# A one-layer decoder trunk on one core: activations' buffers moved by 32 bytes, two weight loads placed behind VectorE's splits, and a last addition cut in two ahead of the final vector's products

## The chip, the cores and the metric

The kernel runs on one core of one Trainium2 chip. The metric is the device time of one execution in microseconds (us). Before the change the median of three runs is 1251.67 us (1251.46 to 1252.79). Differences of about 0.2%, some 2.5 us, are what a measurement of this kernel can tell from no change.

## The reference, cut to what matters

One layer over 256 tokens of width 2048, all in float32:

```
h = rms_norm(x, g_mix);  q,k,v of three head groups = split(h @ w_in)
x += concat(diff_attn(6 heads), block_attn(4), dilated(6)) @ w_out
x += cross_attention(rms_norm(x, g_cross), rms_norm(mem, g_mem)) @ w_co
g, u = split(rms_norm(x, g_ffn) @ w_up)          # 2 x 5632 columns
x += (silu(causal_conv3(g) + b) * u) @ w_down    # 5632 rows
out = rms_norm(x, g_final)
```

Nearly all of the work is the weight matrices: each is read once from HBM and multiplied with 256 tokens.

## The kernel before, in words

**Precision.** Every factor of a product is held as a pair, `hi` and `lo`, in a rounded float32 format (fp32r in the profile): `hi` is the rounded value and `lo` the remainder. A product is then three matmuls: hi by hi, hi by lo, lo by hi. ScalarE makes `hi` of the weights (a copy, L142) and VectorE makes `lo` (a subtraction, L149). The text calls the two together a split.

**Pieces and steps.** The weights come in pieces of 1 MB, each loaded by one DMA of the queue of SP into one of four buffers `raw` (L127). A piece has two halves; half number i is used in step i of the main loop, so that piece k serves the steps 2k and 2k+1. In step i the loop first issues the splits of half i+4 (ScalarE's copy, then work queued for "before step i", then VectorE's subtraction), then TensorE's matmuls of half i, and then work queued for "after step i". Each engine carries out its instructions in just the order in which they are issued, so a split that waits for its load holds up all that is behind it on ScalarE and on VectorE.

**Who stands still in a matmul.** A TensorE matmul loads one factor (the stationary one, 128x128) and streams the other (the moving one). In the products with `w_in`'s q and k columns, `w_out`, `w_cq`, half of `w_ckv` and `w_up`, the weights are stationary and the activations `hT` move: per 128x128 weight block one matmul of 512 columns (L295: `hi` against hi and lo of the activation, side by side) and one of 256 (L302: `lo` against the activation's hi). With `w_co` it is three of 256 columns (L297, L298, L302). For the v columns the activations are stationary and the weights move (L341 to L343, 512 or 256 columns), and in the last product, with `w_down`, the activations `ah` and `al` are stationary and the weights move (L851 to L853, 512 columns). In the cross attention both factors are activations (L401).

**Where the buffers lie.** Each buffer starts at a multiple of 32 bytes in its partition. The weights' buffers `hi`, `lo` and `raw` start at multiples of 64 (`hi` at 67520, 71616 and so on, `lo` at 88000 and so on). Between them and the activations lie many small buffers. `hT` starts at 117856 and 150624, `ah` at 210016, `al` at 214112, all 32 bytes past a multiple of 64, and so do the cross attention's `qk`.

**The start.** By hand, ahead of the loop: x is loaded in pieces between the halves of weight pieces 0, 1 and 2, the splits of halves 0 and 1 are issued, and after steps 0 to 5 come the activations of two more row blocks (`put_x`: L194 on ScalarE, L197 on VectorE) and the splits of halves 2 to 7. The loop itself issues the splits from half 8 on: half 8 in step 4, ahead of `put_x` of the blocks 12 and 13 and of the split of half 6, which come after step 4. A fourth `raw` buffer, `hold`, is set on GpSimd and read by VectorE before step 8, so that no load takes it until then. Piece 3 goes to piece 0's buffer and piece 4 to piece 1's, each when VectorE has split the piece that lay there.

**Evacuation.** A group of four products (4 banks of PSUM) ends every eighth step; its sums leave by a ScalarE copy (L354) and a VectorE addition (L355). Five banks serve the products with `w_in`, so that from its second column group on, the next step's matmuls wait for these.

**The end.** The last two row blocks of `w_down` are kept back, so that the eight column blocks of the output (2 token tiles t, 4 blocks n) end one after another. For each, VectorE adds the residual (L890), ScalarE squares and sums (`square_sum`), and VectorE multiplies with g_final (L898). When all four are in, L899 to L901 add the sums, GpSimd raises to the power -0.5 (L903), and `finish` scales and stores each block.

Of the kernel before, what the change touches and what calls it, by code (L numbers as in the profile page):

```python
# [25 lines left out]
KF = DFF // P  # L26
# [8 lines left out]
HALF = 1024  # L35
NRAW = 4
# [26 lines left out]
def trunk(ctx, tc, x, mem, w_in, w_out, diff_lambda, rel_bias_table, w_cq, w_ckv, w_co, w_up, conv, w_down,  # L63
          g_final, onehot, biasadd, out):
    nc = tc.nc
    PE, DVE, ACT, POOL, SP = nc.tensor, nc.vector, nc.scalar, nc.gpsimd, nc.sync
# [3 lines left out]
    wpool = ctx.enter_context(tc.tile_pool(name="wpool", bufs=1))  # L70
# [35 lines left out]
    pieces = []  # L106
# [6 lines left out]
    def new_raw(p):  # L113
        if p.raw is None:
            p.raw = wpool.tile([P, 2 * HALF], F32, tag="raw", name="raw", bufs=NRAW)

    def load(p):
        new_raw(p)
        at = 0
        for src in p.srcs:  # L120
            n = 1
            for _, c in src.ap[1:]:
                n *= c
            dst = p.raw[:, at:at + n]
            if len(src.ap) == 3:
                dst = dst.rearrange("p (k n) -> p k n", k=src.ap[1][1])
            SP.dma_start(dst, src)  # L127
            at += n
        assert at == 2 * HALF
# [9 lines left out]
    def split_hi(p, h):  # L139
        hi = wpool.tile([P, HALF], F32R, tag="hi", name="hi", bufs=NSPLIT)  # L140
        lo = wpool.tile([P, HALF], F32R, tag="lo", name="lo", bufs=NSPLIT)
        ACT.copy(hi, p.raw[:, h * HALF:(h + 1) * HALF])  # L142
        p.parts[h] = (hi, lo)
        if p.extra is not None and h == 0:
            p.extra[0]()

    def split_lo(p, h):
        hi, lo = p.parts[h]
        DVE.tensor_tensor(lo, p.raw[:, h * HALF:(h + 1) * HALF], hi.bitcast(F32), op=ALU.subtract)  # L149
        if p.extra is not None and h == 0:  # L150
            p.extra[1]()
# [6 lines left out]
    def before(i, f):  # L158
        pre.setdefault(i, []).append(f)

    def after(i, f):
        post.setdefault(i, []).append(f)
# [13 lines left out]
    mhalf = cst.tile([P, 1], F32, name="mhalf")  # L176
# [30 lines left out]
    def xblock(k):  # L207
        return xT[:, k, :]
# [444 lines left out]
    for h in range(HA):  # L653
        i = startA + (0, 6, 11, 17, 22, 28)[h]
# [5 lines left out]
    for j in range(HB):  # L660
        i = startB + (1, 3, 4, 6)[j]
# [161 lines left out]
    def xtok(t, c):  # L823

        return xT[:, 4 * c + 2 * t:4 * c + 2 * t + 2, :].rearrange("p k n -> p (k n)")
# [5 lines left out]
    outs = {}  # L831
    parts = {}
    TAIL = 2
# [9 lines left out]
        hi, lo = parts[k]  # L843
        DVE.tensor_tensor(lo, ffn["a"][:, k, :], hi.bitcast(F32), op=ALU.subtract)

    def down_mm(p, k, h, t, n):
        hi, lo = p.parts[h]
        ah, al = (a[:, t * P:(t + 1) * P] for a in parts[k])
        o = outs[t, 2 * h + n]
        wh, wl = hi[:, n * 512:(n + 1) * 512], lo[:, n * 512:(n + 1) * 512]  # L850
        PE.matmul(o, ah, wh, start=(k == 0), stop=False)  # L851
        PE.matmul(o, ah, wl, start=False, stop=False)  # L852
        PE.matmul(o, al, wh, start=False, stop=(k == KF - 1))  # L853

    ss3 = small(8, "ss3", 1)
    fin = {}

    def finish(n, t, og, r):
        col = slice(n * 512, (n + 1) * 512)
        if t and n % 2:  # L860
            DVE.scalar_tensor_tensor(og[:, col], xtok(t, n), r, gfin["t"][:, col], op0=ALU.mult, op1=ALU.mult)
        elif t or n < 2:
            ACT.activation(og[:, col], og[:, col], AF.Copy, scale=r)
        else:
            (DVE, POOL)[n - 2].tensor_scalar_mul(og[:, col], og[:, col], r)
        SP.dma_start(out[t * P:(t + 1) * P, col], og[:, col])

    def down(k):
        def f(p, h):
            if k == 0 and h == 0:  # L870
                for t in range(NT):
                    for n in range(4):
                        outs[t, n] = any_tile()
            fin[k] = p
            if k < KF - TAIL:
                for t in range(NT):
                    for n in range(2):
                        down_mm(p, k, h, t, n)
            elif k == KF - 1 and h == 1:
                done = None  # L880
                for t in range(NT):
                    og = wpool.tile([P, 2 * HALF], F32, tag="raw", name="raw", bufs=NRAW)
                    ms = small(2, "msf")
                    ss = ss3[:, 4 * t:4 * t + 4]
                    for n in range(4):
                        for kk in range(KF - TAIL, KF):
                            down_mm(fin[kk], kk, n // 2, t, n % 2)
                        col = slice(n * 512, (n + 1) * 512)
                        xc = xtok(t, n)
                        DVE.tensor_tensor(xc, outs[t, n], xc, op=ALU.add)  # L890
                        square_sum(xc, ss[:, n:n + 1])
                        if done:
                            for m in ((3, 0, 1), (2,), (), ())[n]:
                                finish(m, *done)
                        gains = ((), (0,), (), (2,)) if t else ((0,), (1,), (2,), (3,))
                        for m in gains[n]:
                            col = slice(m * 512, (m + 1) * 512)
                            DVE.tensor_tensor(og[:, col], xtok(t, m), gfin["t"][:, col], op=ALU.mult)  # L898
                    DVE.reduce_sum(ms[:, 0:1], ss[:, :3], axis=AX.X)  # L899
                    DVE.tensor_scalar(ms[:, 0:1], ms[:, 0:1], 1.0 / D, EPS, op0=ALU.mult, op1=ALU.add)  # L900
                    DVE.scalar_tensor_tensor(ms[:, 1:2], ss[:, 3:4], 1.0 / D, ms[:, 0:1], op0=ALU.mult, op1=ALU.add)  # L901
                    r = small(1, "rfin")
                    POOL.tensor_tensor(r, ms[:, 1:2], mhalf, op=ALU.pow)  # L903
                    done = t, og, r
                for n in range(4):
                    finish(n, *done)
        return f
# [5 lines left out]
    gfin = {}  # L913
# [8 lines left out]
    def load_x(a, n):  # L922
        c = slice(GCOLS + a * S if a else 0, GCOLS + (a + n) * S)
        SP.dma_start(xin[:, c], x[:, c])

    def load_block(eng, p, k):
        new_raw(p)
        src = p.srcs[0]
        eng.dma_start(p.raw[:, k * 512:(k + 1) * 512],
                      bass.AP(tensor=src.tensor, offset=src.offset + k * src.ap[1][0],  # L930
                              ap=[list(src.ap[0]), list(src.ap[2])]))
# [1 line left out]
    load_x(0, 2)  # L933
    load_block(ACT, pieces[0], 0)
    load_block(SP, pieces[0], 1)
    ACT.copy(small(1, "first", 1), mhalf)
    load_x(2, 2)
    load_half(pieces[0], 1)
    load_x(4, 2)
# [4 lines left out]
    load_half(pieces[2], 0)  # L944
    load_half(pieces[2], 1)
    load_x(12, 4)

    hold = wpool.tile([P, 2 * HALF], F32, tag="raw", name="raw", bufs=NRAW)  # L950
    POOL.memset(hold[:, :1], 0.0)
    before(8, lambda: DVE.tensor_copy(small(1, "held", 1), hold[:, :1]))


    warm = acc_tile()
# [5 lines left out]
    def put_x(k):  # L961
        for f in (high, low):
            for j in range(2):
                f(xblock(k + j), MIX, lambda: hT["h"], k + j)

    def split(i):
        split_hi(pieces[i // 2], i % 2)
        split_lo(pieces[i // 2], i % 2)

    put_x(0)  # L970
    p = pieces[0]
# [5 lines left out]
    put_x(2)  # L977
    split(1)
    load(pieces[3])
    nload = 4  # L980
    for i in range(6):
        after(i, lambda i=i: (put_x(2 * i + 4), split(i + 2)))
    for c in range(4):
        square_part(c + 5, "x", c, lambda c=c: xpart(c))
    norm_factors(10, "x")
# [36 lines left out]
    nsplit = 8  # L1022
    for i in range(2 * len(pieces)):
        cur[0] = i
        new = []
        while nsplit < min(2 * len(pieces), i + 1 + LEAD if i > 2 else 0):
            while nload < len(pieces) and nload <= nsplit // 2 + NRAW - 2:
                load(pieces[nload])
                nload += 1
            new.append((pieces[nsplit // 2], nsplit % 2))  # L1030
            nsplit += 1
        for p, h in new:
            split_hi(p, h)
# [39 lines left out]
```

## Time and profile before

The profile is of one execution of 1252.27 us. Its span, from the first to the last instruction, is 1250.5 us, so 1.77 us lie around it; it is 0.60 us above the median of the runs.

| | |
|---|---|
| median of three runs | 1251.67 us |
| profiled execution | 1252.27 us, span 1250.5 us, mean granted TensorE clock 0.995 |
| matmuls | 6928, busy 1235.8 us |
| VectorE, ScalarE busy | 830.8 us, 630.0 us |
| HBM read | 230 MB, 186 GB/s over the span |

A row of the view of groups gives the source line, engine, operation, `out<-in` by the program's names, sizes, count, then busy time, the mean of one in ns and the idle time ahead. A row of the timeline gives start and duration in us, the instruction, and in brackets how long the engine was idle before it and what ended that. [...]

### The profile page before, as it was taken

The numbers are of one execution on the slowest core, as the hardware profiler recorded it, in microseconds if no ns is written. First come the engines' busy times: TensorE is split into PE (matmuls) and PEld (weight loads), VectorE is DVE, ScalarE is ACT, GpSimd is POOL, SyncE is SP. The second block draws the span as 40 slices with busy tenths as digits, with TensorE's granted clock in tenths as the row PEclk, the third lists the DMA queues.
The fourth block names the chain that finished last, engine by engine and source line by source line (L and its number), as shares of the span: only waits on it lengthen the run. The fifth ranks groups of instructions, "written<-read, shape, count | busy, mean of one in ns | idle before, by whom it ended". The sixth has DMA issues, their size and how long they took to land.

```text
span 1250.5 us, 17611 instructions
## 1 busy us (share of the span) xinstructions
PE 1235.8 (99%) x6928; PEld 1072.4 (86%) x6928; DVE 830.8 (66%) x1351; ACT 630.0 (50%) x979; POOL 12.3 (1%) x23
## 2 busy tenths in 40 slices
PE   8999999999999999999999999999999999999997
PEld 7888888988888899888888888888888888888885
DVE  5755676576568877876767768667776854445445
ACT  6544555556455656545445444444444544444444
POOL 0000000000000000000000000000000000000000
PEclk9999999999999999999999999999999999999998
DMA  7855554555566555565556565565556555555541
GB/s 275 273 172 191 189 170 159 182 184 156 177 227 217 170 169 164 204 206 169 170 201 196 175 202 190 183 201 184 187 180 202 192 193 180 200 176 194 187 150 68
DMA packets 104835, 233.26 MB, mean 187 GB/s; under 512 B 4208, under 2 KB 14768, under 8 KB 98992
## 3 DMA queue, kind: packets, MB, share of 16 engines
q1 hardware_dynamic: 104576, 231.85, 55.3%
q8 instruction: 54, 0.88, 0.3%
q10 hardware_dynamic: 144, 0.26, 0.1%
q14 instruction: 29, 0.24, 0.1%
q0 software_dynamic: 32, 0.02, 0.0%
HBM read 230.00 MB, written 2.12 MB: 186 GB/s over the span
## 4 chain that ended last, share of the span: by engine, by line
issue 58%; PE 37%; DMA 2%; DVE 2%; ACT 0%; POOL 0%; DVEq 0%; POOLq 0%; SPq 0%; ACTq 0%
PE acc L295 16%; PE acc L302 8%; PE acc L341 3%; PE acc L343 3%; PE acc L342 3%; DMA raw<-in_w_in 1%; PE at L401 1%; DMA xin<-in_x 1%; DVE lo L149 1%; PE at L420 0%; PE at L444 0%; DVE hT L197 0%; PE acc L298 0%; PE acc L297 0%; PE at L472 0%
## 5 line engine op out<-in xcount | busy, mean ns | idle before, releaser
L149 DVE TENSOR_TENSOR lo<-raw,hi 128x1024 fp32r<-128x1024 f32 x423 | 517.1, 1223 | 360.0 <-ACT hi L142 359.5
L142 ACT CAST hi<-raw 128x1024 fp32r<-128x1024 f32 x423 | 442.8, 1048 | 473.1 <-PE acc L295 272.4
L295 PE MATMUL acc<-hT,hi 128*128 128x512 f32 x1776 | 625.4, 395 | 3.5 <-ACT hi L142 3.3
L302 PE MATMUL acc<-hT,lo 128*128 128x256 f32 x1840 | 512.0, 280 | 0.6 <-DVE lo L149 0.6
L295 PEld LDWEIGHTS acc<-hT,hi 128*128 128x128 f32 x1776 | 334.4, 188 | 78.1 <-ACT hi L142 3.7
L302 PEld LDWEIGHTS acc<-hT,lo 128*128 128x128 f32 x1840 | 345.3, 188 | 1.4 <-DVE lo L149 1.2
L295 PE MATMUL at<-hT,hi 128*128 128x512 f32 x528 | 187.5, 392 | 0.0
L302 PE MATMUL at<-hT,lo 128*128 128x256 f32 x528 | 147.6, 280 | 0.0
L295 PEld LDWEIGHTS at<-hT,hi 128*128 128x128 f32 x528 | 99.1, 188 | 21.8
L302 PEld LDWEIGHTS at<-hT,lo 128*128 128x128 f32 x528 | 99.2, 188 | 0.0
L851 PE MATMUL acc<-hi,ah 128*128 128x512 f32 x220 | 87.8, 399 | 0.0
L853 PE MATMUL acc<-hi,al 128*128 128x512 f32 x220 | 86.7, 394 | 0.0
L852 PE MATMUL acc<-lo,ah 128*128 128x512 f32 x220 | 86.2, 392 | 0.0
L341 PE MATMUL acc<-hi,hT 128*128 128x256 f32 (+1 forms) x224 | 75.0, 335 | 0.0
L343 PE MATMUL acc<-hi,hT 128*128 128x256 f32 (+1 forms) x224 | 73.9, 330 | 0.0
L342 PE MATMUL acc<-lo,hT 128*128 128x256 f32 (+1 forms) x224 | 73.8, 330 | 0.0
L851 PE MATMUL at<-hi,ah 128*128 128x512 f32 x132 | 52.7, 399 | 0.0
L853 PE MATMUL at<-hi,al 128*128 128x512 f32 x132 | 52.0, 394 | 0.0
L788 ACT ACTIVATE y<-y 128x256 f32<-128x256 f32 x44 | 18.4, 419 | 66.3 <-DVE y L784 66.3
L852 PE MATMUL at<-lo,ah 128*128 128x512 f32 x132 | 51.7, 392 | 0.0
L853 PEld LDWEIGHTS acc<-hi,al 128*128 128x128 f32 x220 | 41.3, 188 | 10.8
L852 PEld LDWEIGHTS acc<-lo,ah 128*128 128x128 f32 x220 | 41.3, 188 | 9.8
(159 smaller groups left out, 1003.2 us busy)
## 6 DMA issues: line engine op xcount, KB each, us to landing
raw<-in_w_up SPq DMA_DIRECT2D x88, 1024.0 KB, 5.0
raw<-in_w_in SPq DMA_DIRECT2D x45, 1024.0 KB, 5.2
raw<-in_w_down SPq DMA_DIRECT2D x44, 1024.0 KB, 4.9
raw<-in_w_out SPq DMA_DIRECT2D x12, 1024.0 KB, 5.3
raw<-in_w_ckv SPq DMA_DIRECT2D x8, 1024.0 KB, 5.6
raw<-in_w_out SPq DMA_DIRECT2D x8, 512.0 KB, 4.9
raw<-in_w_cq SPq DMA_DIRECT2D x4, 1024.0 KB, 5.3
raw<-in_w_co SPq DMA_DIRECT2D x4, 1024.0 KB, 5.2
```

The lines of the kernel that those rows point to most:

```text
L142: ACT.copy(hi, p.raw[:, h * HALF:(h + 1) * HALF])
L149: DVE.tensor_tensor(lo, p.raw[:, h * HALF:(h + 1) * HALF], hi.bitcast(F32), op=ALU.subtract)
L295: PE.matmul(accs[n], w, x, start=(i == 0), stop=False)
L302: PE.matmul(accs[n][:, :S], lo[:, j, n * P:(n + 1) * P], src()[:, korder[i], :S], start=False, stop=(i == len(korder) - 1))
L341: PE.matmul(o, xh, hi[:, j, :], start=(i == 0), stop=False)
L342: PE.matmul(o, xh, lo[:, j, :], start=False, stop=False)
L343: PE.matmul(o, xl, hi[:, j, :], start=False, stop=(i == len(korder) - 1))
L401: PE.matmul(out, a[u], b[w], start=first and i == 0, stop=last and i == 2)
L788: after(cur[0] + 1 + n, lambda: ACT.activation(gate[k], gate[k], AF.Silu))
L851: PE.matmul(o, ah, wh, start=(k == 0), stop=False)
L852: PE.matmul(o, ah, wl, start=False, stop=False)
L853: PE.matmul(o, al, wh, start=False, stop=(k == KF - 1))
```

## The change

Three parts.

1. `ss3` grows from 8 to 10 floats and `first` from 1 to 16, and `held` is gone. With that `hT` starts at 117888 and 150656, `ah` at 210048, `al` at 214144, and `qk` and the other buffers behind move by the same 32 bytes: all at multiples of 64. The weights' buffers stay.
2. `hold` is gone. Piece 3 is loaded into the free fourth buffer at once. Pieces 4 and 5 are loaded after steps 3 and 5, each behind a VectorE instruction that sets one column of the buffer (L999) and that stands behind the split of half 5 and of half 7. The loop loads from piece 6 on, from step 6.
3. At the end, the last column block of the second token tile is computed as two of 256 columns, the second in a bank of its own; its products with g_final are made before the scaling, two of them behind the last additions; `finish` then scales on VectorE and ScalarE by turns, and for the first tile on ScalarE and GpSimd.

```diff
-    ss3 = small(8, "ss3", 1)
+    ss3 = small(10, "ss3", 1)
...
-    ACT.copy(small(1, "first", 1), mhalf)
+    ACT.copy(small(16, "first", 1)[:, :1], mhalf)
...
-    hold = wpool.tile([P, 2 * HALF], F32, tag="raw", name="raw", bufs=NRAW)
-    POOL.memset(hold[:, :1], 0.0)
-    before(8, lambda: DVE.tensor_copy(small(1, "held", 1), hold[:, :1]))
...
     load(pieces[3])
-    nload = 4
+    nload = 6
     for i in range(6):
         after(i, lambda i=i: (put_x(2 * i + 4), split(i + 2)))
+    def load_behind(p):
+        new_raw(p)
+        DVE.memset(p.raw[:, :1], 0.0)
+        load(p)
+    after(3, lambda: load_behind(pieces[4]))
+    after(5, lambda: load_behind(pieces[5]))
...
-            while nload < len(pieces) and nload <= nsplit // 2 + NRAW - 2:
+            while i > 5 and nload < len(pieces) and nload <= nsplit // 2 + NRAW - 2:
                 load(pieces[nload])
...
     def finish(n, t, og, r):
         col = slice(n * 512, (n + 1) * 512)
-        if t and n % 2:
-            DVE.scalar_tensor_tensor(og[:, col], xtok(t, n), r, gfin["t"][:, col], op0=ALU.mult, op1=ALU.mult)
-        elif t or n < 2:
+        if t:
+            if n % 2:
+                ACT.activation(og[:, col], og[:, col], AF.Copy, scale=r)
+            else:
+                DVE.tensor_scalar_mul(og[:, col], og[:, col], r)
+        elif n < 2:
             ACT.activation(og[:, col], og[:, col], AF.Copy, scale=r)
         else:
-            (DVE, POOL)[n - 2].tensor_scalar_mul(og[:, col], og[:, col], r)
+            POOL.tensor_scalar_mul(og[:, col], og[:, col], r)
...
+                    parts_of = ((0, 0, 512), (1, 0, 512), (2, 0, 512)) + (((3, 0, 256), (3, 256, 512)) if t else ((3, 0, 512),))
+                    for i, (n, c0, c1) in enumerate(parts_of):
+                        own = any_tile()[:, :c1 - c0] if c0 else None
...
+                        if own is None:
+                            DVE.tensor_tensor(xtok(t, n), outs[t, n], xtok(t, n), op=ALU.add)
+                        else:
+                            DVE.tensor_tensor(xc, own, xc, op=ALU.add)
...
-                    DVE.scalar_tensor_tensor(ms[:, 1:2], ss[:, 3:4], 1.0 / D, ms[:, 0:1], op0=ALU.mult, op1=ALU.add)
+                    if t:
+                        gained(og, t, 2)
+                        DVE.scalar_tensor_tensor(ms[:, 0:1], ss[:, 3:4], 1.0 / D, ms[:, 0:1], op0=ALU.mult, op1=ALU.add)
+                    DVE.scalar_tensor_tensor(ms[:, 1:2], ss[:, i:i + 1], 1.0 / D, ms[:, 0:1], op0=ALU.mult, op1=ALU.add)
+                    if t:
+                        gained(og, t, 3)
```

What this does to the order is seen at two places on VectorE. The first is the start, before the change. The rows go from the splits of halves 5 and 8 (the first row) over `put_x` of blocks 12 and 13 (L197), the splits of 6 and 9, `put_x` of 14 and 15, and the splits of 7 and 10 and of 11, to the additions that empty the first column group's banks (L355, `mg` is the merged sum; `sq` are sums for the norm).

```order
L149 TENSOR_TENSOR lo<-raw,hi 128x1024 x2
L197 SCALAR_TENSOR_TENSOR hT<-xin,hT 128x256 x2
L149 TENSOR_TENSOR lo<-raw,hi 128x1024 x2
L197 SCALAR_TENSOR_TENSOR hT<-xin,hT 128x256 x2
L149 TENSOR_TENSOR lo<-raw,hi 128x1024 x2
L227 TENSOR_TENSOR sq<-sq 128x1024
L149 TENSOR_TENSOR lo<-raw,hi 128x1024
L355 TENSOR_TENSOR mg<-acc,mg 128x256 x4
```

The same place after the change, from the split of half 5 on:

```order
L149 TENSOR_TENSOR lo<-raw,hi 128x1024
L999 MEMSET raw 128x1
L149 TENSOR_TENSOR lo<-raw,hi 128x1024
L197 SCALAR_TENSOR_TENSOR hT<-xin,hT 128x256 x2
L149 TENSOR_TENSOR lo<-raw,hi 128x1024 x2
L197 SCALAR_TENSOR_TENSOR hT<-xin,hT 128x256 x2
L149 TENSOR_TENSOR lo<-raw,hi 128x1024
L999 MEMSET raw 128x1
L149 TENSOR_TENSOR lo<-raw,hi 128x1024
L227 TENSOR_TENSOR sq<-sq 128x1024
L149 TENSOR_TENSOR lo<-raw,hi 128x1024
L355 TENSOR_TENSOR mg<-acc,mg 128x256 x4
```

Nothing else moved here; the first L999 stands between the splits of halves 5 and 8 and the second between those of halves 7 and 10, and the loads of pieces 4 (halves 8 and 9) and 5 (halves 10 and 11) wait for them. ScalarE's order is the same as before, with the copy of half 8 still ahead of `put_x` of blocks 12 and 13.

The second place is VectorE's end, behind the last matmuls but one block, first before the change (`msf` is the mean square, `raw` the output's buffer):

```order
L890 TENSOR_TENSOR xin<-acc,xin 128x512
L898 TENSOR_TENSOR raw<-xin,gfin 128x512
L899 TENSOR_REDUCE msf<-ss_92 128x1
L900 TENSOR_SCALAR msf<-msf 128x1
L901 SCALAR_TENSOR_TENSOR msf<-ss_92,msf 128x1
L861 SCALAR_TENSOR_TENSOR raw<-xin,rfin,gfin 128x512 x2
```

And after it:

```order
L900 TENSOR_TENSOR xin<-acc,xin 128x512
L902 TENSOR_TENSOR xin<-acc,xin 128x256
L910 TENSOR_REDUCE msf<-ss_92 128x1
L911 TENSOR_SCALAR msf<-msf 128x1
L873 TENSOR_TENSOR raw<-xin,gfin 128x512
L914 SCALAR_TENSOR_TENSOR msf<-ss_92,msf 128x1
L915 SCALAR_TENSOR_TENSOR msf<-ss_92,msf 128x1
L873 TENSOR_TENSOR raw<-xin,gfin 128x512
L864 TENSOR_SCALAR raw<-raw,rfin 128x512 x2
```

The last addition is of 256 columns, one product more stands ahead of the mean square, one behind it, and the two fused scalings became plain ones.

More of the change, by code (lines that the diff above doesn't have):

```diff
@@ L844, in a_low, with down_mm @@
         DVE.tensor_tensor(lo, ffn["a"][:, k, :], hi.bitcast(F32), op=ALU.subtract)
-    def down_mm(p, k, h, t, n):
+    def down_mm(p, k, h, t, n, c0=0, c1=512, own=None):
         hi, lo = p.parts[h]
         ah, al = (a[:, t * P:(t + 1) * P] for a in parts[k])
-        o = outs[t, 2 * h + n]
-        wh, wl = hi[:, n * 512:(n + 1) * 512], lo[:, n * 512:(n + 1) * 512]
-        PE.matmul(o, ah, wh, start=(k == 0), stop=False)
+        o, first = (outs[t, 2 * h + n][:, c0:c1], 0) if own is None else (own, KF - TAIL)
+        wh, wl = (a[:, n * 512 + c0:n * 512 + c1] for a in (hi, lo))
+        PE.matmul(o, ah, wh, start=(k == first), stop=False)
         PE.matmul(o, ah, wl, start=False, stop=False)
         PE.matmul(o, al, wh, start=False, stop=(k == KF - 1))
-    ss3 = small(8, "ss3", 1)
+    ss3 = small(10, "ss3", 1)
     fin = {}
@@ L859, in finish, with gained @@
         col = slice(n * 512, (n + 1) * 512)
-        if t and n % 2:
-            DVE.scalar_tensor_tensor(og[:, col], xtok(t, n), r, gfin["t"][:, col], op0=ALU.mult, op1=ALU.mult)
-        elif t or n < 2:
+        if t:
[4 more added lines that the diff above has]
+        elif n < 2:
             ACT.activation(og[:, col], og[:, col], AF.Copy, scale=r)
         else:
-            (DVE, POOL)[n - 2].tensor_scalar_mul(og[:, col], og[:, col], r)
+            POOL.tensor_scalar_mul(og[:, col], og[:, col], r)
         SP.dma_start(out[t * P:(t + 1) * P, col], og[:, col])
+    def gained(og, t, n):
+        col = slice(n * 512, (n + 1) * 512)
+        DVE.tensor_tensor(og[:, col], xtok(t, n), gfin["t"][:, col], op=ALU.mult)
     def down(k):
@@ L883, in f @@
                     ms = small(2, "msf")
-                    ss = ss3[:, 4 * t:4 * t + 4]
-                    for n in range(4):
+                    ss = ss3[:, 5 * t:5 * t + 5]
+                    parts_of = ((0, 0, 512), (1, 0, 512), (2, 0, 512)) + (((3, 0, 256), (3, 256, 512)) if t else ((3, 0, 512),))
+                    for i, (n, c0, c1) in enumerate(parts_of):
+                        own = any_tile()[:, :c1 - c0] if c0 else None
                         for kk in range(KF - TAIL, KF):
[L887 to L891, printed above, removed]
+                            down_mm(fin[kk], kk, n // 2, t, n % 2, c0, c1, own)
+                        xc = xtok(t, n)[:, c0:c1]
+                        if own is None:
+                            DVE.tensor_tensor(xtok(t, n), outs[t, n], xtok(t, n), op=ALU.add)
+                        else:
+                            DVE.tensor_tensor(xc, own, xc, op=ALU.add)
+                        square_sum(xc, ss[:, i:i + 1], c1 - c0)
@@ L892, in f @@
                         if done:
-                            for m in ((3, 0, 1), (2,), (), ())[n]:
+                            for m in ((2, 0), (3, 1), (), (), ())[i]:
                                 finish(m, *done)
[L895 to L898, printed above, removed]
+                        if not t or n < 2:
+                            gained(og, t, n)
```

## The prediction

> **What bounds the kernel now.** I read the page's busy times first, then who TensorE waited for, then the timeline of the start and of the end, then the distance between matmul starts in each kind of product.
>
> ```profile
> span 1250.5 us, 17611 instructions
> PE 1235.8 (99%) x6928; PEld 1072.4 (86%) x6928; DVE 830.8 (66%) x1351; ACT 630.0 (50%) x979; POOL 12.3 (1%) x23
> ```
>
> TensorE is the bound nearly everywhere. So only three things can move the end: the rate of its stream, the places where it stands still, and what follows its last matmul. The view of waits, for TensorE alone, shows one stall within the stream (columns: total us, times, longest):
>
> ```profile
> PE acc L295 <- ACT hi L142: 3.3, 1, 3.3
> PE acc L302 <- DVE lo L149: 0.6, 1, 0.6
> ```
>
> It is at the start. The timeline there, of ScalarE, VectorE and TensorE:
>
> ```profile
> 17.78 1.22 DVE L149 TENSOR_TENSOR lo<-raw,hi 128x1024 fp32r<-128x1024 f32 x1
> 23.85 1.05 ACT L142 CAST hi<-raw 128x1024 fp32r<-128x1024 f32 x1 [6.29 <-DMA raw<-in_w_in]
> 25.61 1.98 ACT L142 CAST hi<-raw 128x1024 fp32r<-128x1024 f32 x2
> 26.70 0.79 PE L295 MATMUL acc<-hT,hi 128*128 128x512 f32 x1 [3.34 <-ACT hi L142]
> 29.93 2.56 DVE L149 TENSOR_TENSOR lo<-raw,hi 128x1024 fp32r<-128x1024 f32 x2
> 32.40 1.22 DVE L227 TENSOR_TENSOR sq<-sq 128x1024 f32<-128x1024 f32 x1
> 33.87 1.23 DVE L149 TENSOR_TENSOR lo<-raw,hi 128x1024 fp32r<-128x1024 f32 x1 [0.25 <-ACT hi L142]
> 35.02 1.50 DVE L355 TENSOR_TENSOR mg<-acc,mg 128x256 f32<-128x256 f32 x4
> 36.18 0.39 PE L295 MATMUL acc<-hT,hi 128*128 128x512 f32 x1
> ```
>
> ScalarE's copy of half 8 (23.85) waits for piece 4's load, and the copy of half 6 (25.61), which TensorE needs for step 6, stands behind it. The stall also costs clock, as the view by windows shows (the granted clock is the third number from the end, 0.50; DMA share and GB/s follow it):
>
> ```profile
> 26.70:32.30 5.60, 4.95 (x14) 3.87 (x15) 5.49 (x7) 5.48 (x7) 0.00 (x0) 0.50 0.34 91
> ```
>
> For 5.6 us after it the clock was at half.
>
> **Part 1, the loads behind VectorE.** The loads in question, by the view of the tile `raw` in narrow windows: piece 4's, issued at 14.45 into a full queue, and one issued at 29.25 with the queue empty. The second row of each pair gives its time from issue to landing.
>
> ```profile
> 14.45 0.37 SPq L127 DMA_DIRECT2D raw<-in_w_in  x1
> DMA to landing us min/median/max: 9.3/9.3/9.3
> 29.25 0.37 SPq L127 DMA_DIRECT2D raw<-in_w_in  x1
> DMA to landing us min/median/max: 5.3/5.3/5.3
> ```
>
> Piece 4 landed at 14.45 + 9.3 = 23.75. Now it is issued behind half 5's split, which ends at 17.78 + 1.22 = 19.0, plus a one-column write (0.1 as I take it). The queue is then nearly empty, so it lands 5.3 later, at 24.4. The first stall therefore stays and grows by 0.65; nothing in ScalarE's order was changed that could end it. Piece 3's earlier load gains nothing, as half 6 stands behind half 8.
>
> Piece 5 is the dearer one. Before, it was loaded long ahead, and VectorE went from half 7's split to half 10's without a pause (the row at 29.93 holds both). Now its load is issued when half 7's split is done: 29.93 + 1.22 + 0.65 + 0.1 = 31.9, and it lands at 37.2. Queued behind that wait are, on ScalarE, half 10's copy (1.05), on VectorE half 10's split, a sum of squares, half 11's split (about 1.15 each from start to start, 3.45 together), and behind them the additions L355. Four of them (1.50 together) must empty the banks that step 8 needs. The first would end at 37.2 + 0.1 + 1.05 + 3.45 + 0.4 = 42.2. TensorE came to the second block of step 8 at 36.18 before; there it would now stand until 42.2, so it is 6.0 us late. The first stall's 0.65 is a part of these, not an addition. On SP's queue the loads from piece 6 on and five small ones stand behind piece 5's; their buffers are free, so piece 6 is issued at once and has landed when ScalarE, after 42, comes to its first half.
>
> The new stall of over 5 us should halve the clock again. The nearest row is the one above: 5.6 us at half, 2.8 us lost. How much of the spell falls inside the stall I cannot tell, so I take 2.4, between 0 and 2.8. Part 1: **+8.4 us**, between +6.0 and +9. [...]
>
> GpSimd's write to `hold`, ahead of the warm-up, and VectorE's read of it cost nothing either way: the first real matmul waits for activations, and the read (0.14) stood behind L355.
>
> **Part 2, the alignment.** In a stream the cost of a matmul is the distance between starts. Between the first two rows lie twelve matmuls of 256 columns, between the next two twelve more of 256, then sixteen pairs of 512 and 256, then twenty-four of 512; the last row, of the chain, counts six of 256:
>
> ```profile
> 479.64 0.28 PE L297 MATMUL acc<-hT,hi 128*128 128x256 f32 x1
> 481.05 0.28 PE L297 MATMUL acc<-hT,hi 128*128 128x256 f32 x1
> 104.09 0.28 PE L341 MATMUL acc<-hi,hT 128*128 128x256 f32 x1
> 105.53 0.28 PE L341 MATMUL acc<-hi,hT 128*128 128x256 f32 x1
> 600.18 0.28 PE L302 MATMUL at<-hT,lo 128*128 128x256 f32 x1
> 605.73 0.28 PE L302 MATMUL at<-hT,lo 128*128 128x256 f32 x1
> 1100.55 0.40 PE L851 MATMUL acc<-hi,ah 128*128 128x512 f32 x1
> 1106.15 0.40 PE L851 MATMUL acc<-hi,ah 128*128 128x512 f32 x1
> 455.02 0.72 PE acc L401 x6
> ```
>
> Per matmul, at 256 columns: with aligned weights standing and unaligned activations moving (L297, L298, L302) 1.41 / 12 = 117.5 ns; the other way round (L341 to L343) 1.44 / 12 = 120 ns; with both unaligned (L401) 0.72 / 6 = 120 ns. So it is the unaligned stationary factor that goes with the slower rate, by 2.5 ns, and whether the moving one is aligned does not show. At 512 columns likewise: a pair of L295 and L302, weights standing, takes 5.55 / 16 = 346.9 ns, of which 229.4 are the 512 columns if the 256 take 117.5; L851 to L853, activations standing, take 5.60 / 24 = 233.3, which is 3.9 more. I take 2.5, the like-for-like figure at one width, for all matmuls whose stationary factor is moved. Their groups on the page:
>
> ```profile
> L342 PE MATMUL acc<-lo,hT 128*128 128x256 f32 (+1 forms) x224 | 73.8, 330 | 0.0
> L852 PE MATMUL acc<-lo,ah 128*128 128x512 f32 x220 | 86.2, 392 | 0.0
> L852 PE MATMUL at<-lo,ah 128*128 128x512 f32 x132 | 51.7, 392 | 0.0
> ```
>
> With their two sister lines each, 3 x (224 + 220 + 132) = 1728 matmuls: **-4.3 us**, between 0 and -6.7 (3.9 each). No stream in this trace has both factors aligned, so the other 2304 pairs of L295 and L302 are unpriced; I take 0 for them and leave the rest to the rivals.
>
> **Part 3, the end.** The timeline behind the last matmul:
>
> ```profile
> 1241.45 0.69 DVE L890 TENSOR_TENSOR xin<-acc,xin 128x512 f32<-128x512 f32 x1 [0.52 <-PE acc L853]
> 1242.06 0.68 DVE L898 TENSOR_TENSOR raw<-xin,gfin 128x512 f32<-128x512 f32 x1
> 1243.10 0.16 DVE L901 SCALAR_TENSOR_TENSOR msf<-ss,msf 128x1 f32<-128x1 f32 x1
> 1239.25 0.48 DVE L865 TENSOR_SCALAR raw<-raw,rfin 128x512 f32<-128x512 f32 x1
> 1243.95 1.42 DVE L861 SCALAR_TENSOR_TENSOR raw<-xin,rfin,gfin 128x512 f32<-128x512 f32 x2 [0.69 <-POOL rfin L903]
> 1243.95 1.33 ACT L863 ACTIVATE raw<-raw,rfin 128x512 f32<-128x512 f32 x2 [1.00 <-POOL rfin L903]
> 1244.70 1.80 SPq L866 DMA_DIRECT2D out<-raw  x4
> ```
>
> Twelve matmuls of 256 at 120 ns in place of six of 512 at 233.3: +0.04. The last addition, of 256 columns, takes about 0.4 (as L355's do) instead of 0.69, but one product (0.6 from start to start) still stands ahead of the mean square, and the mean square now takes one more small step (some 0.2): its last step starts near 1243.1 again, so the shorter addition is given back. What is left is the scaling: 0.48 on VectorE, where the first block was ScalarE's half of 1.33, so the four stores, which are issued one after another, begin 0.2 sooner. Part 3: **-0.2 us**, between -0.5 and +0.3. The first token tile's second GpSimd scaling lies beside the second tile's matmuls.
>
> **The sum.** 1252.27 + 8.4 - 4.3 - 0.2 = 1256.2 on the profiled execution, which lies 0.6 above the median: **1255.6 us**, slower by 0.3%. With the bounds of the terms this case reaches from 1250 (+6.0 - 6.7 - 0.5) to 1258.5 (+9.0 - 2.5 + 0.3). What a measurement can tell from no change is 0.2%, 2.5 us.
>
> **The rivals.**
>
> (a) *An aligned moving factor is faster too.* 2304 pairs have an unaligned one now. At the same 2.5 ns a matmul that is 4608 x 2.5 = 11.5 us more, and the time 1244.1; it decides from 0.85 ns a matmul on, where it outweighs the sum of +3.9. For it speaks that in no row are both aligned; against it that aligning the moving factor made no difference between L341 and L401, and that L851's is aligned and slow. At 5 ns it would be 1232.6. [...]
>
> (b) *The alignment changes nothing*, and the rates differ for what the products are. Then 1259.9. [...] The row of 117.5 against 120 speaks against it.
>
> (c) *It is the aligned moving factor that is slow* in L851. Then L295 goes from 229.4 to 233.3: 2304 x 3.9 = +9.0, no gain elsewhere: 1268.9.
>
> (d) *The stall in step 8 does not come*, if piece 5's load is not held where I read it, so that only the 0.65 of the first one is left: 1251.67 + 0.65 - 4.3 - 0.2 = 1247.8. The order of VectorE speaks against it.
>
> **How the numbers follow.** The forecast has 0.36, (a) 0.29, (b) 0.20, (c) 0.07, (d) 0.08. Faster: (a) but 0.01 of it, and (d) but 0.01, 0.35. Within 0.2%: these 0.02 and a quarter of the forecast's case, whose clock loss is smallest, 0.11. Slower: the rest, 0.54. The range takes (d), (b) with its bounds, the forecast, and (a) down to about 4 ns a matmul, 1237 to 1262; beyond it lie a quarter of (a) and all of (c), 0.15. The forecast's own range is 1250 to 1258.5.
>
> **What would show it.** In the profile after: ScalarE's copy of half 8 starts near 24.5 and TensorE's stall there is 3.3 to 4.1 us; a second stall of 5 to 6.5 us follows near 36 to 42, ended by VectorE's L355, with PEclk 0.50 behind it; a gap of 6 to 7 us stands between VectorE's second one-column write and half 10's split. L851 to L853 take about 230.8 ns, L341 to L343 117.5 at 256 columns, and 16 pairs of L295 and L302 5.55 us as before. If the pairs take under 5.50 us, (a) holds and I am wrong on the side of slower; if TensorE has no second stall, part 1 is wrong; if L851 stays at 233.3, part 2 is.

## The result, and the profile after

The changed kernel takes 1266.95 us (median of four runs, 1266.66 to 1267.8) against 1251.57 us before in the same rounds. The ratio is 1.012 with a 95% interval of 1.0105 to 1.0135: slower by 15.4 us, where the prediction said 1255.6 and a range up to 1262. The direction was right, the size was not.

The head of the page after, and the view of waits for TensorE (total us, times, longest):

```profile
span 1265.2 us, 17634 instructions
PE 1244.3 (98%) x6934; PEld 1076.1 (85%) x6934; DVE 832.5 (66%) x1355; ACT 631.7 (50%) x981; POOL 14.6 (1%) x23
```

```profile
PE acc L295 <- DVE mg L355: 5.4, 1, 5.4
PE acc L295 <- ACT hi L142: 3.5, 1, 3.5
PE acc L302 <- DVE lo L149: 0.7, 1, 0.7
```

The first stall is still there, and there is a second one of 5.4 us behind VectorE's additions. The span is 14.7 us longer, and these waits are only 5.7 us of it (9.6 in place of 3.9). The timeline shows how the second stall comes about:

```profile
31.39 0.06 DVE L999 MEMSET raw<- 128x1 f32 x1
36.92 1.04 ACT L142 CAST hi<-raw 128x1024 fp32r<-128x1024 f32 x1 [6.33 <-DMA raw<-in_w_in]
38.00 1.23 DVE L149 TENSOR_TENSOR lo<-raw,hi 128x1024 fp32r<-128x1024 f32 x1 [6.55 <-ACT hi L142]
41.41 1.41 DVE L355 TENSOR_TENSOR mg<-acc,mg 128x256 f32<-128x256 f32 x4
41.88 0.80 PE L295 MATMUL acc<-hT,hi 128*128 128x512 f32 x1 [5.39 <-DVE mg L355]
45.89 0.40 PE L295 MATMUL acc<-hT,hi 128*128 128x512 f32 x1
```

The one-column write starts at 31.39, piece 5's load is behind it, ScalarE idles 6.33 us for that load, VectorE 6.55 us for ScalarE, and TensorE goes on at 41.88, where before it passed this place at 36.18. The view by windows has the clock behind it (granted clock third from the end):

```profile
41.80:45.30 3.50, 3.42 (x11) 2.94 (x12) 3.50 (x7) 2.10 (x3) 0.00 (x0) 0.50 0.87 285
```

TensorE's matmuls of 512 columns, which take 0.80 and then 0.63 us in this stretch, are back at their usual 0.40 us at 45.89. So behind 5.39 us of idling the granted clock was 0.50 for 4.0 us.

The rest lies in the stream itself. Its matmuls overlap (a row of L851 lasts 0.39 us and the next starts 0.23 us behind it), so their cost is read from the distances between starts. The timeline of TensorE after, a row and the one 16 pairs of L295 and L302 later, and two rows of L851 with 24 matmuls between:

```profile
600.13 0.40 PE L295 MATMUL acc<-hT,hi 128*128 128x512 f32 x1
605.78 0.40 PE L295 MATMUL at<-hT,hi 128*128 128x512 f32 x1
1100.38 0.39 PE L851 MATMUL at<-hi,ah 128*128 128x512 f32 x1
1105.87 0.39 PE L851 MATMUL at<-hi,ah 128*128 128x512 f32 x1
```

A pair takes 5.65 / 16 = 353.1 ns; before it was 346.9. A matmul of L851 to L853 takes 5.49 / 24 = 228.8 ns; before it was 233.3. So one product became faster, as forecast, and the other slower, which the forecast had priced at nothing.

And the end, on VectorE and GpSimd:

```profile
1255.43 0.28 PE L853 MATMUL acc<-hi,al 128*128 128x256 f32 x1
1255.38 0.68 DVE L900 TENSOR_TENSOR xin<-acc,xin 128x512 f32<-128x512 f32 x1
1256.17 0.42 DVE L902 TENSOR_TENSOR xin<-acc,xin 128x256 f32<-128x256 f32 x1
1257.69 0.68 DVE L873 TENSOR_TENSOR raw<-xin,gfin 128x512 f32<-128x512 f32 x1
1257.86 0.95 POOL L919 TENSOR_TENSOR rfin<-msf,mhalf 128x1 f32<-128x1 f32 x1 [1.33 <-DVE msf L915]
```

The last addition starts 0.74 us behind the last matmul's start (0.44 before), not soon behind its end: an addition of 512 columns (1255.38) is still ahead of it.

### The profile page after: what moved, and what is told of

It reads as the page before. It is cut to its first block, busy times and chain, and to the rows that moved or that the text cites. A ratio compares the mean times of both kernels' runs of the same rounds, so it can differ in the third digit from the quotient of the medians.

```text
span 1265.2 us, 17634 instructions
## 1 busy us (share of the span) xinstructions
PE 1244.3 (98%) x6934; PEld 1076.1 (85%) x6934; DVE 832.5 (66%) x1355; ACT 631.7 (50%) x981; POOL 14.6 (1%) x23
## 4 chain that ended last, share of the span: by engine, by line
issue 58%; PE 38%; DMA 2%; DVE 1%; POOL 0%; ACT 0%; SPq 0%; POOLq 0%; ACTq 0%; DVEq 0%
PE acc L295 16%; PE acc L302 9%; PE acc L343 3%; PE acc L341 3%; PE acc L342 3%; DMA raw<-in_w_in 2%; PE at L401 1%; PE acc L297 1%; PE acc L298 1%; DVE lo L149 1%; PE at L420 0%; PE at L444 0%; PE at L472 0%; POOL raw L868 0%; ACT hi L142 0%
## 5 line engine op out<-in xcount | busy, mean ns | idle before, releaser
L295 PE MATMUL acc<-hT,hi 128*128 128x512 f32 x1776 | 637.7, 401 | 9.3 <-DVE mg L355 5.4
L302 PE MATMUL acc<-hT,lo 128*128 128x256 f32 x1840 | 515.3, 282 | 0.7 <-DVE lo L149 0.7
L295 PEld LDWEIGHTS acc<-hT,hi 128*128 128x128 f32 x1776 | 335.6, 189 | 92.1 <-DVE mg L355 5.7
L302 PEld LDWEIGHTS acc<-hT,lo 128*128 128x128 f32 x1840 | 346.3, 189 | 1.4 <-DVE lo L149 1.2
L295 PE MATMUL at<-hT,hi 128*128 128x512 f32 x528 | 190.9, 398 | 0.0
L302 PE MATMUL at<-hT,lo 128*128 128x256 f32 x528 | 148.4, 281 | 0.0
L295 PEld LDWEIGHTS at<-hT,hi 128*128 128x128 f32 x528 | 99.3, 188 | 24.5
L302 PEld LDWEIGHTS at<-hT,lo 128*128 128x128 f32 x528 | 99.1, 188 | 0.0
L853 PE MATMUL acc<-hi,al 128*128 128x512 f32 (+1 forms) x222 | 87.0, 392 | 0.0
L852 PE MATMUL acc<-lo,ah 128*128 128x512 f32 (+1 forms) x222 | 86.6, 390 | 0.0
L851 PE MATMUL acc<-hi,ah 128*128 128x512 f32 (+1 forms) x222 | 85.7, 386 | 0.0
L341 PE MATMUL acc<-hi,hT 128*128 128x256 f32 (+1 forms) x224 | 73.9, 330 | 0.0
L343 PE MATMUL acc<-hi,hT 128*128 128x256 f32 (+1 forms) x224 | 73.3, 327 | 0.0
L853 PE MATMUL at<-hi,al 128*128 128x512 f32 x132 | 52.0, 394 | 0.0
L851 PE MATMUL at<-hi,ah 128*128 128x512 f32 x132 | 51.2, 388 | 0.0
L851 PEld LDWEIGHTS acc<-hi,ah 128*128 128x128 f32 x222 | 41.7, 188 | 9.2
```

The costliest lines, as they stand in the source:

```text
L295: PE.matmul(accs[n], w, x, start=(i == 0), stop=False)
L302: PE.matmul(accs[n][:, :S], lo[:, j, n * P:(n + 1) * P], src()[:, korder[i], :S], start=False, stop=(i == len(korder) - 1))
L341: PE.matmul(o, xh, hi[:, j, :], start=(i == 0), stop=False)
L343: PE.matmul(o, xl, hi[:, j, :], start=False, stop=(i == len(korder) - 1))
L851: PE.matmul(o, ah, wh, start=(k == first), stop=False)
```

## The experiments

Theory A was formed from the two traces: each factor's own place matters, an aligned moving factor slows the pairs, an aligned stationary one speeds up the other products. Rival B was that the loads' new order slows the stream. Later theories are named where they came up. Where several kernels ran together, they share the runs of the kernel before.

**Loads and end, without the alignment.**

```diff
 (the changed kernel)
-    ACT.copy(small(16, "first", 1)[:, :1], mhalf)
+    ACT.copy(small(1, "first", 1), mhalf)
```

> Parts 1 and 3 of the change (loads and end) with the activations' buffers at their old place, 32 bytes past a multiple of 64. Theory A (the address sets the rates: an aligned moving factor slows the pair of L295 and L302 by 6.67 ns, an aligned stationary one speeds up the others by about 4.4): a pair takes 346.7 ns and L851 233.3 as before, the stall in step 8 is 5 to 6 us as in the changed kernel, the start costs 7.7 us and the end 0.3, so 1259.6 us. Rival B (the pairs got slower from the loads' new order or the clock behind it, not from the addresses): pairs stay at 353.3, and the time is about 1267 plus the lost gain of the other products, 1272 to 1275.

Measured 1260.45 against 1252.53 us, ratio 1.0062 (1.0049 to 1.0076): +7.9 us. The pairs are at 346.7 ns and L851 to L853 at 233.3, so rival B falls. Two rows with 16 pairs from the first to the second:

```profile
700.27 0.39 PE L295 MATMUL acc<-hT,hi 128*128 128x512 f32 x1
705.82 0.39 PE L295 MATMUL acc<-hT,hi 128*128 128x512 f32 x1
```

**The alignment alone.**

```diff
 (the kernel before)
-    ACT.copy(small(1, "first", 1), mhalf)
+    ACT.copy(small(16, "first", 1)[:, :1], mhalf)
```

> Only part 2: the buffers from hT on moved by 32 bytes, loads and end as before. Theory A: pairs 353.3 ns, L851 228.9, one stall of 3.3 us at the start as before; net +6 to +8 us, 1258 to 1259.5. Rival B: pairs 346.7 and L851 228.9: 1244 to 1247.5. The forecast's own price (0 for the pairs, -2.5 for the others): 1247.3.

Measured 1258.92 against 1252.53, ratio 1.0051 (1.0038 to 1.0063): +6.4 us. Its timeline again has 16 pairs in 5.65 us:

```profile
600.24 0.40 PE L295 MATMUL at<-hT,hi 128*128 128x512 f32 x1
605.89 0.40 PE L295 MATMUL at<-hT,hi 128*128 128x512 f32 x1
```

So 32 bytes of place, with no other edit, slowed the pairs by 6.7 ns (353.3 in place of 346.7). The two runs together give 14.3 of the 15.4 us.

**Streams alone, a first try.** A kernel that only fills buffers and runs 39 short streams of 16 or 24 matmuls (behind four to warm up), at offsets of the two factors.

```diff
+    for name, kind, s, s2, m in STREAMS:
+        acc = psum.tile([P, 512], F32, tag="acc", name=name, bufs=8)
+        for i in range(8):
+            if kind == "P":
+                hi, lo, mv = SH + s + 512 * i, SL + s2 + 512 * i, MOV + m + 2048 * (i % 4)
+                PE.matmul(acc, a(hi, P), a(mv, 512), start=True, stop=True)
+                PE.matmul(acc[:, :256], a(lo, P), a(mv, 256), start=True, stop=True)
```

> Streams of matmuls alone, without other work: pairs (P) of 512 and 256 columns, triples of 512 with the activations standing (D), triples of 256 with the activations standing (V, and W at the second activation buffer's place) or the weights standing (C); s is the stationary factor's offset in bytes past a multiple of 64, m the moving one's, l the offset of the second stationary factor where it differs. The output is not computed. Theory A: P takes 353 ns at every m0 and 347 at m32, whatever s; D takes 687 at s0 and 700 at s32, whatever m. Rival C (what counts is whether both lie alike): P is slow at s0_m0 and s32_m32 alike and fast at s0_m32 and s32_m0. Rival D (other engines' traffic makes the difference): no difference between any of them.

P took 351.8 ns a pair at s0_m0 and 352.0 at s32_m32, and 347 at s0_m32 and s32_m0; D 686.7 at s0_m0 and s32_m32, 700 at s32_m0 and 701.5 at s0_m32. That is rival C's pattern: both alike against both different. Theory A falls, and rival D too, since no other engine is at work. But a repeat of s0_m32 at the end gave 352.5: a stream of eight pairs did not give the same rate twice.

**The grid.** The same, with 32 pairs in the kernel's own order to a stream.

```diff
-for _s in (0, 16, 32, 48):
-    for _m in (0, 16, 32, 48):
+for _s in range(0, 64, 8):
+    for _m in range(0, 64, 8):
```

> Streams of matmuls alone, long enough to settle: 32 pairs per stream in the kernel's own order (four groups of 128 columns, two row blocks each) at each of 8 x 8 offsets of the stationary (s) and the moving factor (m) past a multiple of 64 bytes, then triples with the activations standing (D 512 columns, V 256) at 4 x 4. The output is not computed. Theory A (the moving factor's own offset decides in the pairs, the stationary one's in the triples): columns m0 of P all at 353.3 ns, m32 all at 346.7; D depends on s alone. Theory C (what counts is the distance of the two modulo 64): P is 353.3 where s = m and 346.7 where they differ by 32; D and V are fast where s = m (686.7, 340) and slow where they differ by 32 (700, 360).

Theory A fell for good: in column m0 the pairs took 346.7 to 353.9 ns, in column m32 the same. But C did not hold either: s0_m32 took 353.9 and s32_m0 346.7, though both are 32 apart modulo 64. The triples kept C's pattern at the offsets 0 and 32 (686.7 ns where s and m agree, 700 where they do not), but at s16_m16, where the two agree as well, they took 680.0. The first matmul of the stream and of the one behind it, 16 triples later, for s0_m0 and then for s16_m16:

```profile
765.33 0.39 PE L131 MATMUL D_s_m<-arena 128*128 128x512 f32 x1
776.32 0.39 PE L131 MATMUL D_s_m<-arena 128*128 128x512 f32 x1
820.84 0.39 PE L131 MATMUL D_s_m<-arena 128*128 128x512 f32 x1
831.73 0.39 PE L131 MATMUL D_s_m<-arena 128*128 128x512 f32 x1
```

The rows give 686.9 and 680.6 ns with each stream's start in them.

**Both moved by 32 bytes, in the kernel.**

```diff
 (the kernel before; lo likewise)
-        hi = wpool.tile([P, HALF], F32R, tag="hi", name="hi", bufs=NSPLIT)
+        hi = wpool.tile([P, HALF + 16], F32R, tag="hi", name="hi", bufs=NSPLIT)[:, 8:8 + HALF]
```

> The kernel before, with the weights' hi and lo moved by 32 bytes as well, so that both factors lie 32 bytes past a multiple of 64 everywhere. Theory A: moving hT is off 64 as before, so a pair stays at 346.7 ns; the standing ah is off too, 233.3: the time is that of before. Theory C: both lie alike, so the rates are those of the changed kernel: pair 353.3, L851 228.9, L341 faster, +6.4 us as in the run with the alignment alone.

Measured 1249.66 against 1252.02, ratio 0.9978 (0.9968 to 0.9987); the pairs of the products with `w_up` averaged 346.5 ns. C asked for 353.3. The buffers now lie 64 bytes further apart than before, one to the next, and so the rate changed from buffer to buffer. In one of them seven pairs took 2.38 us, 340 ns a pair; these are the starts of the first, the second and the eighth:

```profile
574.72 0.39 PE L296 MATMUL at<-hT,hi 128*128 128x512 f32 x1
575.06 0.39 PE L296 MATMUL acc<-hT,hi 128*128 128x512 f32 x1
...
577.10 0.40 PE L296 MATMUL at<-hT,hi 128*128 128x512 f32 x1
```

**Only `ah` and `al` moved.**

```diff
 (the kernel before; al likewise)
-        hi = f.tile([P, S], F32R, tag="ah", name="ah", bufs=4)
+        hi = f.tile([P, S + 16], F32R, tag="ah", name="ah", bufs=4)[:, 8:8 + S]
```

> The kernel before, with only ah and al moved by 32 bytes, so that they lie like the weights, and hT as before. Theories A and C both: L851 to L853 at 228.9 in place of 233.3, 1056 of them, -4.7 us, pairs at 346.7 as before: 1247.9 against 1252.5. If the gain of the triples needs hT moved as well: no change.

Measured 1249.84 against 1252.02, ratio 0.9979 (0.997 to 0.9988): half the gain that was expected. Triples of L851 to L853 averaged 692.2 ns and took from 680 to 709, changing from one of the four buffers to the next. These too lie 64 bytes further apart than before, so all four have the same distance to the weights modulo 64 and yet not the same rate. If it is a distance that counts, it must be one modulo more than 64: theory E.

**The scan of distances.** Streams over distances d modulo 512, always counted in bytes from the weights to the activations, and over e, a shift of the second stationary factor. The weights stay where they are.

```diff
+for _e, _step in ((0, 16), (32, 32), (64, 32), (128, 32), (256, 32)):
+    for _d in range(0, 512, _step):
+        STREAMS.append((f"P_d{_d}_e{_e}", "P", 0, _d, _e, 4))
+for _e in (0, 64, 128, 256):
+    for _d in range(0, 512, 32):
+        STREAMS.append((f"D_d{_d}_e{_e}", "D", _d, 0, _e, 16))
```

> Streams of matmuls alone as in the grid, now over all distances d (in bytes, modulo 512) from the first stationary weights to the moving activations (P, C), or from the weights to the standing activations (D; V by its activations), and e, the distance of the second stationary factor (lo, or al) beyond its place in the kernel. The output is not computed. Theory E (the rate follows the distance modulo 128 or more, not modulo 64): P at d160 (before) 346.7, at d192 (after) 353.3, and d96, d224, d288 that agree with one of them modulo 64 give other values; somewhere 340 is met, as in some stretches of the run with both moved; D at d160 700, at d192 686.7, at some d 680. Theory C (modulo 64 only): P repeats every 64 bytes, 346.7 at every d that is 32 past a multiple of 64.

The timeline at the first matmul of a stream and of the one behind it: P at d160 (the place before), at d192 (the place after) and at d64 with e64, each with 32 pairs between; then D at d0, and at d160 and d192, which follow on one another, each with 48 matmuls.

```profile
155.86 0.40 PE L120 MATMUL P_d_e<-arena 128*128 128x512 f32 x1
166.96 0.39 PE L120 MATMUL P_d_e<-arena 128*128 128x512 f32 x1
178.16 0.39 PE L120 MATMUL P_d_e<-arena 128*128 128x512 f32 x1
189.45 0.39 PE L120 MATMUL P_d_e<-arena 128*128 128x512 f32 x1
603.78 0.39 PE L120 MATMUL P_d_e<-arena 128*128 128x512 f32 x1
614.67 0.40 PE L120 MATMUL P_d_e<-arena 128*128 128x512 f32 x1
1117.87 0.39 PE L138 MATMUL D_d_e<-arena 128*128 128x512 f32 x1
1128.78 0.39 PE L138 MATMUL D_d_e<-arena 128*128 128x512 f32 x1
1173.57 0.40 PE L138 MATMUL D_d_e<-arena 128*128 128x512 f32 x1
1184.77 0.40 PE L138 MATMUL D_d_e<-arena 128*128 128x512 f32 x1
1195.77 0.40 PE L138 MATMUL D_d_e<-arena 128*128 128x512 f32 x1
```

The rows give 346.9, 352.8 and 340.3 ns a pair, and 681.9, 700.0 and 687.5 ns a triple, with each stream's first groups in them; the settled halves read as follows.

| settled ns of a pair (P) or triple (D) | d0 | d32 | d64 | d96 | d128 | d160 | d192 | d224 |
|---|---|---|---|---|---|---|---|---|
| P, e0 | 353.8 | 346.6 | 353.5 | 350.0 | 350.8 | 346.6 | 353.4 | 346.7 |
| P, e64 | 346.7 | 348.9 | 340.0 | 346.7 | 346.6 | 353.3 | 350.0 | 346.6 |
| D, e0 | 680.0 | 700.0 | 700.0 | 702.5 | 697.9 | 700.0 | 686.6 | 700.0 |

From d256 on the rows repeat themselves within 0.2 ns, with one exception (P at d256, e0: 346.7). Over the places shown, P at e256 repeats P at e0 within 0.7 ns, with one exception too (d224: 353.4). So in this scan, with the weights in one place and but for these two values, the rates came back after 256 bytes: of the activations' distance from the weights, and of the second stationary factor's from the first. In the row P at e0, the places that are 32 past a multiple of 64 do mostly win, which is why modulo 64 looked right; at e64 and in D they do not.

The table also accounts for the two runs before it. By the addresses that the program gives its buffers, the run with both moved has d0, d64, d128 and d192 among its five weight buffers, all at e64. Its pairs with `w_up` averaged 347.2, 341.5, 346.9 and 350.0 ns there (pairs held up by other work left out), and the row has 346.7, 340.0, 346.6 and 350.0. With only `ah` and `al` moved, their four buffers lie at d192, d0, d64 and d128; the triples averaged 687.6, 682.8, 699.6 and 698.4, and the row has 686.6, 680.0, 700.0 and 697.9.

The distances are not the whole rule, though. In the grid both factors moved, and s0_m0 and s16_m16 have the same distance and yet 686.7 and 680.0 ns. Likewise pairs at distance 160 took 346.7 at s32_m0 and 353.3 at s40_m8, and triples of 256 columns with the activations standing 353.4 at s0_m0 and 340.0 at s32_m32. What else counts was not tried.

**The splits of half 8 behind those of half 7.**

```diff
 (the kernel before)
-        while nsplit < min(2 * len(pieces), i + 1 + LEAD if i > 2 else 0):
+        while nsplit < min(2 * len(pieces), i + 1 + LEAD if i > 5 else 0):
```

> The kernel before, with the splits of halves 8, 9 and 10 issued before step 6 and not from step 4 on, so that ScalarE's copy of half 6 no longer stands behind the copy of half 8 and its load. If the first stall is that order's doing, as the prediction said, TensorE's 3.3 us and the 0.65 behind it go, and with them the half clock of 5.6 us (2.8 us lost): 1246 to 1248. Rival (the load of piece 3 or the activations end it too): the stall only shrinks, 1249 to 1252.

Measured 1248.11 against 1252.38, ratio 0.9972 (0.9961 to 0.9983). The stall in front of step 6 is gone, and one of 2.1 us takes its place in step 8. VectorE now has the splits of halves 8 to 11 one close behind another, ahead of the additions (the row of three, and the one at 30.45):

```profile
25.91 3.50 DVE L149 TENSOR_TENSOR lo<-raw,hi 128x1024 fp32r<-128x1024 f32 x3 [0.49 <-ACT hi L142]
30.45 1.22 DVE L149 TENSOR_TENSOR lo<-raw,hi 128x1024 fp32r<-128x1024 f32 x1
31.59 1.41 DVE L355 TENSOR_TENSOR mg<-acc,mg 128x256 f32<-128x256 f32 x4
```

```profile
PE acc L295 <- DVE mg L355: 2.1, 1, 2.1
```

**Piece 5's load behind half 5's split.**

```diff
 (the run with loads and end)
-    after(5, lambda: load_behind(pieces[5]))
+    after(3, lambda: load_behind(pieces[5]))
```

> The run of loads and end without the alignment (1260.5), but with piece 5's load placed behind half 5's split, like piece 4's. If the load behind half 7's split makes the stall in step 8, as part 1 says, that stall goes and the first one stays: 1252.5 to 1254. If the stall has another cause (the evacuation's own order): 1260 again.

Measured 1253.45 against 1252.38, ratio 1.0007 (0.9998 to 1.0017), 7 us less than with the load behind half 7's split. Only the first stall is left of the two:

```profile
PE acc L295 <- ACT hi L142: 3.8, 1, 3.8
```

**Places from the scan, in the kernel.**

```diff
 (the kernel before)
-        lo = wpool.tile([P, HALF], F32R, tag="lo", name="lo", bufs=NSPLIT)
+        lo = wpool.tile([P, HALF + 64], F32R, tag="lo", name="lo", bufs=NSPLIT)[:, p.off:p.off + HALF]
...
-        hi = f.tile([P, S], F32R, tag="ah", name="ah", bufs=4)
+        hi = f.tile([P, S + 64], F32R, tag="ah", name="ah", bufs=4)[:, 48:48 + S]
...
-    ACT.copy(small(1, "first", 1), mhalf)
+    ACT.copy(small(48, "first", 1)[:, :1], mhalf)
```

Here `off` is 16 floats for the pairs' pieces and 0 for the others, and `al` is treated like `ah`.

> The kernel before with nothing but places changed, chosen from the scan: the activations hT 64 bytes from the weights' hi modulo 256, the lo of the pairs' weights 64 bytes further than before (d64, e64), ah and al at the weights' own place modulo 256 (d0). Theory E (the distances modulo 256 set the rate, in the kernel as in the bare streams): a pair 340.0 ns, three of L851 to L853 680.0, so 2304 x 6.67 and 352 x 20 ns less, -22.4 us, and 1 to 2 us more from the v columns: 1228 to 1230.5 against 1252.4. Theory C (distance modulo 64): hT and hi both at a multiple of 64, so pairs at 353.3 as in the changed kernel, 1258.

Measured 1231.76 against 1252.35, ratio 0.9836 (0.9823 to 0.985): -20.6 us with no instruction changed but in its addresses. The timeline has 16 pairs in 5.44 us and eight triples in 5.44 us:

```profile
699.76 0.39 PE L295 MATMUL at<-hT,hi 128*128 128x512 f32 x1
705.20 0.39 PE L295 MATMUL at<-hT,hi 128*128 128x512 f32 x1
1099.97 0.39 PE L851 MATMUL at<-hi,ah 128*128 128x512 f32 x1
1105.41 0.39 PE L851 MATMUL at<-hi,ah 128*128 128x512 f32 x1
```

That is 340.0 and 680.0 ns, as the scan had them, where C asked for pairs at 353.3. The time is over the forecast's 1230.5 all the same. By the distances between starts L851 to L853 gained 7.0 us, as forecast, and the v columns 1.6, but the pairs 11.8 in place of 15.4. In the first 450 us some 200 pairs ran near 350, which is 2.0 us of what is missing; the rest was not traced.

**Places, and splits in a better order at the start.**

```diff
 (the run with the places)
-        while nsplit < min(2 * len(pieces), i + 1 + LEAD if i > 2 else 0):
+        while nsplit < min(2 * len(pieces), i + 1 + (LEAD if i > 7 else 2) if i > 5 else 0):
```

> The same, and the splits of halves 8 and 9 one step each ahead of steps 6 and 7, those of 10 to 12 before step 8, so that neither the copy of half 6 nor the additions that empty the first banks stand behind a split that waits. If both stalls of the start (3.3 us before, 2.1 in the run with the splits before step 6) come from that order, none over 0.7 us is left: 5.5 to 7 us less than the run with the places alone, 1222 to 1224.5.

Measured 1226.13 against 1252.35, ratio 0.9791 (0.9777 to 0.9804): -26.2 us, the fastest of all. That is 5.6 us less than with the places alone, within the 5.5 to 7 that were forecast, though over the forecast time as that run was. No stall of TensorE behind a split is over 0.2 us:

```profile
PE at L241 <- DVE sq L236: 1.3, 1, 1.3
PE acc L295 <- ACT hi L142: 0.2, 1, 0.2
```

## Why the prediction was wrong, point by point

- **Part 1, the start: right.** It said that piece 4 would be waited for at 24.4, the copy of half 6 would still stand behind, and TensorE would stand before the second block of step 8 until 42.2. It stood until 41.88. The one-column write, taken at 0.1 us without a row, took 0.06. The clock behind it was at half for 4.0 us, some 1.9 lost. Forecast +8.4; the run with loads and end has +7.9, with the end's few tenths in it. That piece 5's load is the cause is shown by the run that moves only that load (7.0 us less).
- **Part 2, the stationary factors: right in sign, too small, for the wrong reason.** The forecast was 1728 matmuls faster by 2.5 ns, -4.3 us. L851 to L853 gained (700.0 - 686.7) / 3 = 4.4 each, -4.7 us over 1056, and L341 to L343 gained 3.9 to 4.4 each: -7.5 in all, beyond the bound of -6.7. That the sign came right is luck: in the row D at e0 only d0 and d192 lie more than 3 ns below the 700 of before, and the change happened to go to d192.
- **Part 2, the pairs: the step that failed.** It was "No stream in this trace has both factors aligned, so the other 2304 pairs of L295 and L302 are unpriced; I take 0 for them". They became slower by 353.3 - 346.7 = 6.7 ns each, 15.4 us. The case with this sign, an aligned moving factor that is slow, had a chance of 0.07 and 9.0 us, and no gain elsewhere. Net of the gains that makes 7.9; the run of the alignment alone measures +6.4 (4.8 to 7.9 by its interval), and its last matmul starts 6.65 us later (the first row is before):

```profile
1241.01 0.40 PE L853 MATMUL acc<-hi,al 128*128 128x512 f32 x1
1247.66 0.40 PE L853 MATMUL acc<-hi,al 128*128 128x512 f32 x1
```

By the distances between starts in these two traces the other products gained 7.4 us, and the pairs took 13.9 us more and not 15.4. So what is missing is missing among the pairs; why is open.

- **The step behind it.** The prediction read 117.5 against 120 ns as a price of the stationary factor's own alignment, since the moving one's seemed to make no difference. The three products differ in which buffers meet, and so in their distances; in the first try the rate went with the combination (D took 686.7 ns at s0_m0 and at s32_m32, 700 at s32_m0 and 701.5 at s0_m32). With one trace of one placement no factor could be given a price of its own, and an unpriced term of 2304 pairs was the largest in the sum: at the 2.5 to 5 ns a matmul that the rivals used, it was 11 to 23 us either way. The range reached up only 6.4 us above the forecast. (The forecast's own upper bound of 1258.5 also takes -2.5 for part 2, where its stated bound is 0; with 0 it would be 1261.0.)
- **Part 3, the end: wrong sign, small.** Forecast -0.2; the trace has +0.3 from the last matmul's start to the end of the span (9.77 us in place of 9.49). The first half of the last column block still has an addition of 512 columns, which the prediction did not count; it ends at 1256.06, just ahead of the last one (1256.17). From the last addition's start to the end of the mean square it took 1.61 us in place of 1.81, and from the scaling's start to the end of the span, with the stores, 6.35 in place of 6.55, but GpSimd's power took 0.95 us beside a VectorE product, and before, beside none, 0.57:

```profile
1243.35 0.57 POOL L903 TENSOR_TENSOR rfin<-msf,mhalf 128x1 f32<-128x1 f32 x1 [3.15 <-DVE msf L901]
1252.29 0.55 POOL L919 TENSOR_TENSOR rfin<-msf,mhalf 128x1 f32<-128x1 f32 x1 [727.49 <-DVE msf L915]
```

The second row is the first tile's power in the changed kernel. It ran beside a VectorE addition that reads PSUM (L900, from 1252.13) and took no longer. In the other two runs with this end (loads and end, and piece 5's load) the last power took 0.95 us again, beside the same product. Whether the product is the reason was not tried.

## What to carry to other kernels

When an edit moves the buffers that TensorE reads, the sum has a term for every stream that reads them, and its size comes from the number of matmuls (here 2304 pairs at 6.7 ns), even where its sign is unknown: give that term both signs in the range. Here the place of one operand alone set no rate (in the scan d160 gave 346.6 ns a pair at e0 and 353.3 at e64); measure the pair of places, in a bare stream of the kernel's own order, choose both together, and check the rate in the kernel, since the same places did not always give the same one (353.3 and 340.0 ns for L297, L298 and L302). And a load that was put behind VectorE's work held up what stood behind its consumer on three engines (ScalarE idled 6.33 us, VectorE 6.55, TensorE 5.39), which could be read off the order before any run.

## What the runs showed of the hardware

- At a granted clock of 1.00, with nothing else at work, the same pair of matmuls of 512 and 256 columns took from 340.0 to 353.9 ns, and a triple of 512 columns from 680.0 to 702.5, in streams that differ in addresses alone. With the weights in one place the rates at d256 and beyond were those at d0 to d224 within 0.2 ns, and those of pairs at e256 were those at e0 within 0.7, with the exceptions named. The rates 340.0, 346.7 and 353.3 lie 6.67 ns apart, with others between them (350.0); what such a step is, no run here says.
- The same places ran at two rates. The three matmuls of L297, L298 and L302 took 353.3 ns in the run with the places and 340.0 in the one with the better start, at the same addresses, and the scan has 353.4 at their distance. Pairs at s0_m32 took 347 in the first try and 353.9 in the grid, and some 200 pairs of the run with the places 350 where the others took 340. What decides between them, no run here shows.
